# Forming the Strassen sums of w_out in the first phase and during the merges instead of in attention, and loading A11 of the out-projection during the last merge

## The chip, the cores and the metric

The kernel runs on one core of one Trainium2 chip. The metric is the device time of one execution in microseconds (us); several runs are taken and their median is given. The profile is of one execution, with a time of its own. Engines: PE (TensorE: matmuls; PEld its weight loads), DVE (VectorE), ACT (ScalarE), POOL (GpSimd), SP (SyncE, which issues all of this kernel's transfers, in one queue).

## The reference

One layer of a decoder trunk on 1024 tokens and 16 meta tokens, all in float32:

```python
h = rmsnorm(x, gain)
zin = h @ w_in.astype(h.dtype)                      # 2048 x 10240
q, k, v, g_attn, u, g_pool, m_attn, m_pool = jnp.split(zin, cuts, axis=-1)
o_attn = stick_breaking_attention(q, k, v).reshape(B, L, SB_WIDTH)
o_attn = (o_attn * jax.nn.silu(g_attn.astype(jnp.float32))).astype(x.dtype)
y_attn = o_attn @ w_attn_up.astype(x.dtype)         # 1024 x 2048
pooled = multiscale_pool(u.astype(jnp.float32))
mixed = jnp.einsum('blgc,gcd->blgd', pooled, pool_w.astype(jnp.float32)).reshape(B, L, POOL_WIDTH)
o_pool = (mixed * pool_scale.astype(jnp.float32) * jax.nn.silu(g_pool.astype(jnp.float32))).astype(x.dtype)
y_pool = o_pool @ w_pool_up.astype(x.dtype)         # 1024 x 2048
merged = jax.nn.sigmoid(m_attn) * y_attn + jax.nn.sigmoid(m_pool) * y_pool
return x + merged @ w_out.astype(x.dtype)           # 2048 x 2048
```

The layer's output goes through a last rmsnorm, and the meta tokens are dropped. The attention weights are `sigmoid(z) * product of (1 - sigmoid(z))` over the keys between, which the kernel forms by a running product (a scan) along the keys.

## The kernel before, in words

**Numbers.** Each float32 operand is split into a high and a low part (`split`, L115: ACT writes the high part at L116, DVE or POOL the rest at L117), and each product is three matmuls (`mm3`, L137, or L1007 to L1009): high x high, high x low, low x high. 512 columns are one matmul, so a block of 128 x 2048 by 2048 x 512 tokens is made of many of them.

**Products.** The two large projections, by w_in and by w_out, save multiplications in Strassen's manner: with each matrix cut in four, seven products of sums of quarters take the place of eight. So sums of quarters of the weights are needed (`make_sums`, L266, for w_in; `w_forms`, L183, for w_out), sums of quarters of the inputs, and sums of the results. Columns of w_in are worked on in pairs of 128, a `Duo` each; there are 40 of them.

**Stages**, by the profile's clock:

1. *First phase* (0 to about 985 us). The norm and the transposed input; six early duos; then the loop over `rest` (n = 0 to 33), in which each duo takes four of its seven products: by X0, X2, X1 and X3. For each duo the raw blocks of w_in are loaded (`load_raw`, L249, tiles raw0 with two buffers, raw1 and rawb with one each), POOL makes eight sums of them (L271), four of which go to DRAM (d_r, L280), and ACT and DVE split the others. Results go to DRAM as d_nu (L296, after X2), d_c or d_sa and d_sp (L314, after X1), d_up (L301, after X3). The pool p0 (small vectors of the norm and one tile `st` for early results) stays open for the whole phase; the pool wa (rawb, the sums, `st`, `tm`) lies beside it, over the memory of the pool px that is closed by then.
2. *Pooling* (to about 1170 us). The other three products of the pooling duos, the causal pooling and its group maps.
3. *Attention* (to about 1910 us). For each of eight heads the other three products of its two duos, and the attention itself as a generator that is advanced one step every few matmuls: scores, mask (L748 on POOL), scan (L753 on DVE), transpose (L769), values. Between them the remaining products of the 16 gate duos. `duo` and `silu_duo` call `between[0]` after each product; that advances `w_forms`.
4. *Merges* (to about 2275 us). 32 products of 128 output channels by the up-projections, in a written order of ("p", c) and ("a", c) pairs: the gate from DRAM is multiplied with the product (L965, L970), and the attention part added to the pool part on POOL (L971). When both halves of a channel pair are there, `sums` makes four sums (L949), and seven tiles go to DRAM (d_f, L957).
5. *Out-projection* (to the end). `prod` takes the seven products; A11 is loaded first, through the tile mr with two buffers (`fill_f`, L1013), the other operands (A12, R2, R3, and later R1, A22, R4) one block per step of the products before.

**w_forms before.** For each half p of w_out's columns, each of eight row blocks j and each half i of 512 columns it loads four blocks (tiles cw0 to cw3, 256 columns, 128 KB each), makes three of the four forms by subtractions on POOL (L194) and stores them (L195), loads two more blocks and makes the fourth: six loads, four subtractions, four stores, in three steps. 32 such units are spread over attention.

**Order of the work.** The framework orders the instructions of each engine by its own plan, not strictly by the source: what is ready may go ahead. `tc.keep_in_program_order` ties an instruction behind the one traced before it on its engine, so that it can't go ahead of that one; later ones can still go ahead of it. A new tile whose memory lay in a closed pool waits for the users of the tiles that were there (`reuse_waits="tile"`). A queue runs in the order that was planned, and an instruction that waits holds what is behind it.

Of the kernel before, what the change touches and what calls it, by code (L numbers as in the profile page):

```python
# [9 lines left out]
F32 = mybir.dt.float32  # L10
# [5 lines left out]
P = 128  # L16
D = 2048
KC = D // P
# [17 lines left out]
HALF = SEQ // 2  # L36
# [36 lines left out]
def trunk_kernel(  # L73
# [14 lines left out]
    nc = tc.nc  # L88
# [22 lines left out]
    def nm(s):  # L111
        uid[0] += 1
        return f"{s}_{uid[0]}"
# [66 lines left out]
    def w_form(n):  # L180
        return lambda p, j: d_wf[n][p][:, j * 512 : (j + 1) * 512]

    def w_forms(pool):  # L183

        for p, j, i in ((p, j, i) for p in range(2) for j in range(KH) for i in range(2)):
            c = slice(i * 256, (i + 1) * 256)

            def block_of(tag, kh, nh):
                t = pool.tile([P, 256], F32, tag=tag, name=nm("cw"), bufs=1)
                tc.keep_in_program_order(nc.sync.dma_start(t, w_block(p, j, kh, nh)[:, c]))  # L190
                return t

            def minus(n, a, b):
                tc.keep_in_program_order(nc.gpsimd.tensor_tensor(out=a, in0=a, in1=b, op=ALU.subtract))  # L194
                tc.keep_in_program_order(nc.sync.dma_start(w_form(n)(p, j)[:, c], a))  # L195
# [33 lines left out]
    with ExitStack() as actx:  # L229
# [15 lines left out]
        with ExitStack() as xctx:  # L245
# [68 lines left out]
                nc.sync.dma_start(dst, t)  # L314

            X0, X1 = xquads(0, XW), xquads(1, XW)
            p0 = xctx.enter_context(tc.tile_pool(name="p0", bufs=2, side="right", reuse_waits="tile"))
            gk = p0.tile([P, KC], F32, tag="gk", name="gk", bufs=1)
            early = ALL[:6]
            ops = {}  # L320
# [10 lines left out]
            with tc.tile_pool(name="px", bufs=1, side="right", reuse_waits="tile") as px:  # L331
# [94 lines left out]
                for d in early[1:]:  # L426
                    early_ops(d, 0)
                    a = acc_tile()
                    for kq in range(KQ):
                        block([a], WHOLE, X0, kq, ops[d.n, 0, kq], True)  # L430
                    s1 = wr_tile()
                    nc.scalar.activation(s1, a, AF.Copy)
                    nc.sync.dma_start(d_nu[d.n], s1)
                    early_ops(d, 1)
                    for kq in range(KQ):
                        block([a], WHOLE, X1, kq, ops[d.n, 1, kq], False)
                        if d.n < 5:
                            last_tokens(2 * (d.n - 1) + kq)
                    out_c(p0, 1, d, [a], WHOLE)
            nc.sync.dma_start(psc, pool_scale.rearrange("(c p) -> p c", p=P))  # L440

            wa = xctx.enter_context(tc.tile_pool(name="wa", bufs=1, side="right", reuse_waits="tile"))
# [58 lines left out]
            early_rest(early[0])  # L501
            raws = all_raws(rest[0])
            r2, r3 = make_sums(wa, rest[0], raws, SB)
            for n, d in enumerate(rest):
                pieces = WITHM if d.meta else WHOLE
                a, b = [acc_tile() for _ in pieces], acc_tile()
                for kq in range(KQ):
                    block(a, pieces, X0, kq, op_of(c0(raws[0][kq])), True)
                s1 = copy_p1(wa, STB, a, pieces)
                for kq in range(KQ):  # L510
                    block([b], WHOLE, X2, kq, op_of(r2[kq]), True)
                out_nu(wa, STB, d, s1, b)
                for kq in range(KQ):
                    block(a, pieces, X1, kq, op_of(c0(raws[1][kq])), False)
                out_c(wa, STB, d, a, pieces)
                m7 = [op_of(r3[kq]) for kq in range(KQ)]
                last = d is rest[-1]
                more = n + 1 < len(early)
                if not last and not more:
                    raws = all_raws(rest[n + 1])  # L520
                    r2, r3 = make_sums(wa, rest[n + 1], raws, SB)
                for kq in range(KQ):
                    block([b], WHOLE, X3, kq, m7[kq], False)
                out_up(wa, STB, d, s1, b)
                if more:
                    if n + 2 < len(early):
                        fetch_s1(early[n + 2])
                    early_rest(early[n + 1])
                    raws = all_raws(rest[n + 1])
                    r2, r3 = make_sums(wa, rest[n + 1], raws, SB)  # L530
                if 7 <= n < 7 + KC // 2:
                    second_operands(n - 7)
                if n == 7 + KC // 2:
                    second_meta()
                if 6 <= n < 6 + KC // 2:
                    fetch_x22(n - 6)

        def load_wr(src):
            raw = wp.tile([P, 512], F32, tag="wr", name=nm("wr"), bufs=4)
# [82 lines left out]

            return m5, n4, p3

        between = [lambda: None]

        def duo(*args):
            for call in duo_steps(*args):
                call()
                between[0]()  # L630

        def tok_tile(pool, tag, dt):

# [7 lines left out]
        with ExitStack() as a0ctx:  # L641
# [24 lines left out]
            def silu_duo(*args):  # L666
                for call in silu_steps(*args):
                    call()
                    between[0]()
# [51 lines left out]
        with tc.tile_pool(name="a1", bufs=1, side="right", reuse_waits="tile") as a1:  # L721
# [124 lines left out]
                duo(d, dst, post, None, step)  # L846

            gates = [d for d in ALL if d.kind in ("ma", "mp")]
            forms = w_forms(a1)
            between[0] = lambda: next(forms, None)  # L850
            for h in range(HEADS):
                d = named["kv", h]
                vT = tok_tile(a1, "vT", F32)
# [34 lines left out]
            for _ in att:  # L888
                pass
            gate_duo(gates.pop(0), None)  # L890
            for _ in forms:
                pass

    xo = ctx.enter_context(tc.tile_pool(name="xo", bufs=1, reuse_waits="tile"))
    xc = ctx.enter_context(tc.tile_pool(name="xc", bufs=1, side="right", reuse_waits="tile"))
# [10 lines left out]
    with tc.tile_pool(name="pm", bufs=2, side="right", reuse_waits="tile") as pm:  # L906
# [28 lines left out]
        for n, k in enumerate((("p", 0), ("p", KH), ("p", 1))):  # L935
            order.remove(k)
            order.insert(n, k)
        op, oa = [xquads(0, HALF, xo), xquads(1, HALF, xo)], [xquads(2, HALF), xquads(3, HALF, xc)]
        for t in range(2):
            fill_up(op[t], d_op, t)  # L940
# [2 lines left out]
        def sums(j):  # L943
# [9 lines left out]
            r3 = add(a11, a21)  # L953
            r2 = add(r1, a11)
            r4 = add(r2, a12)
            for n, t in enumerate((a11, a12, r2, r3, r1, a22, r4)):
                nc.sync.dma_start(d_f[n][j], t)  # L957

        for n, (kind, c) in enumerate(order):
            if n in (0, 1):  # L960
                fill_up(oa[n], d_oa, n)
            if kind == "p":
                gs = [gate("sp", 6, d_sp, c, t) for t in range(2)]
                for t, a in up_mm(w_pu, op, c):
                    nc.vector.tensor_tensor(out=gs[t], in0=a, in1=gs[t], op=ALU.mult)  # L965
                sps[c] = gs
            else:
                gs = [gate("sa", 6, d_sa, c, t) for t in range(2)]
                for t, a in up_mm(w_au, oa, c):
                    nc.vector.tensor_tensor(out=gs[t], in0=a, in1=gs[t], op=ALU.mult)  # L970
                    nc.gpsimd.tensor_tensor(out=gs[t], in0=gs[t], in1=sps[c][t], op=ALU.add)  # L971
                ms[c] = gs
                if c >= KH:
                    sums(c - KH)

    pr = ctx.enter_context(tc.tile_pool(name="pr", bufs=2, side="right", reuse_waits="tile"))
    rows = [[], []]
# [207 lines left out]
```

## Time and profile before

| | |
|---|---|
| time, median of three runs | 2611.47 us (2610.23 to 2613.19) |
| the profiled execution's own time | 2615.75 us |
| its span, from the first to the last instruction | 2614.0 us |
| mean granted clock of TensorE | 0.983 |
| busy: PE, DVE, ACT, POOL | 94%, 48%, 34%, 40% |
| DMA, mean over the span | 178 GB/s |

A busy share is the time in which the engine had an instruction in work, as a share of the span. The matmuls overlap, so that one is shown with about 0.39 us while the next starts 0.23 us later; what is lost on PE is seen in the stretches in which it has nothing in work. In the list of waits a row reads: who waited, for whom, total us, how many times, the longest. In a timeline: start, duration, engine, line, operation, output and inputs, count, and in brackets how long the engine had been idle and what ended that. SPq is the queue of transfers; its rows give the time of issuing, not of landing. In a chain of waits each row is a start, a length and what was on the path.

### The profile page before, as it was taken

How to read it: one execution, taken by the hardware profiler on the slowest of the kernel's cores; microseconds unless marked ns; L12 is line 12 of the kernel's file. 1: busy time of each engine (PE TensorE's matmuls, PEld its weight loads, DVE VectorE, ACT ScalarE, POOL GpSimd, SP SyncE). 2: the span in 40 equal slices, each digit the busy share in tenths (PEclk: the TensorE clock that was granted, in tenths of full speed). 3: DMA queues.
4: the chain of work that ended last, by engine and by line, in shares of the span. 5: the costliest groups of instructions: out<-in, count | busy, mean ns of one | idle time of the engine just before them, and what ended most of it. 6: DMA issues, size and time to landing. Idle time of an engine off the chain costs nothing. (4 is left out here: it accounts for less than half of the span.)

```text
span 2614.0 us, 36254 instructions
## 1 busy us (share of the span) xinstructions
PE 2468.5 (94%) x12680; PEld 2088.1 (80%) x12680; DVE 1253.8 (48%) x2089; ACT 896.0 (34%) x1845; POOL 1034.6 (40%) x962
## 2 busy tenths in 40 slices
PE   6898999999999999899999999999889999899998
PEld 5676778888888887887887888888768888677887
DVE  5432234543333344675575566557652222255456
ACT  6421122222222234224454454445441111044243
POOL 1665555554454534235445544554303222210212
PEclk8999999999999999999999999999989999999999
DMA  5566555665555557436556656554575444375544
GB/s 179 162 206 214 192 192 204 216 226 180 182 182 177 185 186 219 126 126 187 178 174 183 187 165 191 182 177 141 164 239 173 138 143 135 116 238 185 183 132 169
DMA packets 418168, 466.24 MB, mean 178 GB/s; under 512 B 35505, under 2 KB 278577, under 8 KB 416945
## 3 DMA queue, kind: packets, MB, share of 16 engines
q1 hardware_dynamic: 417984, 463.93, 55.8%
q8 instruction: 99, 1.62, 0.3%
q14 instruction: 85, 0.69, 0.1%
HBM read 321.50 MB, written 142.31 MB: 177 GB/s over the span
## 5 line engine op out<-in xcount | busy, mean ns | idle before, releaser
L138 PE MATMUL acc<-x,wh 128*128 128x512 f32 (+2 forms) x2736 | 980.2, 359 | 27.6 <-ACT wh L116 18.5
L140 PE MATMUL acc<-x,wl 128*128 128x512 f32 (+2 forms) x2736 | 971.1, 355 | 8.9 <-DVE wl L117 7.5
L139 PE MATMUL acc<-x,wh 128*128 128x512 f32 (+2 forms) x2736 | 968.8, 354 | 0.0
L138 PEld LDWEIGHTS acc<-x,wh 128*128 128x128 f32 x2736 | 520.1, 190 | 98.6 <-ACT wh L116 24.2
L140 PEld LDWEIGHTS acc<-x,wl 128*128 128x128 f32 x2736 | 518.6, 190 | 86.4 <-DVE wl L117 14.5
L139 PEld LDWEIGHTS acc<-x,wh 128*128 128x128 f32 x2736 | 519.3, 190 | 62.8
L116 ACT ACTIVATE wh<-wr 128x512 fp32r<-128x512 f32 x408 | 256.4, 630 | 580.6 <-PE accb L139 273.2
L117 DVE TENSOR_TENSOR wl<-wr,wh 128x512 fp32r<-128x512 f32 x288 | 217.2, 756 | 241.4 <-ACT wh L116 230.2
L117 DVE TENSOR_TENSOR wl<-r,wh 128x512 fp32r<-128x512 f32 x160 | 150.4, 944 | 339.3 <-ACT wh L116 315.2
L271 POOL TENSOR_TENSOR r<-raw,raw 128x512 f32<-128x512 f32 x80 | 111.7, 1396 | 378.8 <-DMA raw<-in_w_in_dram 357.0
L116 ACT ACTIVATE wh<-r 128x512 fp32r<-128x512 f32 x160 | 100.3, 632 | 469.7 <-POOL r L271 363.8
L117 POOL TENSOR_TENSOR wl<-wr,wh 128x512 fp32r<-128x512 f32 x120 | 171.8, 1431 | 224.0 <-ACT wh L116 170.6
L271 POOL TENSOR_TENSOR r<-r,raw 128x512 f32<-128x512 f32 x160 | 221.4, 1384 | 12.5 <-DMA raw<-in_w_in_dram 2.5
L138 PE MATMUL accb<-x,wh 128*128 128x512 f32 x512 | 200.5, 392 | 12.4 <-ACT x L116 12.4
L139 PE MATMUL accb<-x,wh 128*128 128x512 f32 x512 | 200.7, 392 | 0.0
L140 PE MATMUL accb<-x,wl 128*128 128x512 f32 x512 | 200.2, 391 | 0.0
L1007 PE MATMUL accb<-wh,x 128*128 128x512 f32 x416 | 163.8, 394 | 15.6 <-ACT x L116 13.3
L753 DVE TENSOR_TENSOR_SCAN wt<-wt 128x272 f32<-128x272 f32 (+5 forms) x128 | 109.8, 858 | 142.9 <-POOL wt L748 105.0
L194 POOL TENSOR_TENSOR cw<-cw,cw 128x256 f32<-128x256 f32 x128 | 106.1, 829 | 172.5 <-DMA cw<-in_w_out_dram 152.4
L1009 PE MATMUL accb<-wl,x 128*128 128x512 f32 x416 | 164.0, 394 | 2.5 <-DVE wl L117 2.3
L1008 PE MATMUL accb<-wh,x 128*128 128x512 f32 x416 | 163.3, 393 | 0.0
L971 POOL TENSOR_TENSOR sa<-sa,sp 128x512 f32<-128x512 f32 x32 | 47.2, 1475 | 275.4 <-DVE sa L970 265.9
(176 smaller groups left out, 3124.0 us busy)
## 6 DMA issues: line engine op xcount, KB each, us to landing
raw<-in_w_in_dram SPq DMA_DIRECT2D x96, 512.0 KB, 6.0
d_r<-r SPq DMA_DIRECT2D x160, 256.0 KB, 2.0
wr<-d_r SPq DMA_DIRECT2D x160, 256.0 KB, 3.3
raw<-in_w_in_dram SPq DMA_DIRECT2D x152, 256.0 KB, 5.3
cw<-in_w_out_dram SPq DMA_DIRECT2D x192, 128.0 KB, 3.2
wr<-in_w_in_dram SPq DMA_DIRECT2D x80, 256.0 KB, 3.0
d_wf<-cw SPq DMA_DIRECT2D x128, 128.0 KB, 2.0
wr<-d_wf SPq DMA_DIRECT2D x64, 256.0 KB, 2.8
```

Of the source, the lines that this page charges most:

```text
L116: nc.scalar.activation(hi, src, AF.Copy)
L117: (eng or nc.vector).tensor_tensor(out=lo, in0=src, in1=hi.bitcast(F32), op=ALU.subtract)
L138: nc.tensor.matmul(ps, wh, rh, start=first, stop=False, skip_group_check=skip)
L139: nc.tensor.matmul(ps, wh, rl, start=False, stop=False, skip_group_check=skip)
L140: nc.tensor.matmul(ps, wl, rh, start=False, stop=last, skip_group_check=skip)
L194: tc.keep_in_program_order(nc.gpsimd.tensor_tensor(out=a, in0=a, in1=b, op=ALU.subtract))
L271: nc.gpsimd.tensor_tensor(out=t, in0=a, in1=b, op=ALU.add)
L753: nc.vector.tensor_tensor_scan(out=rev, data0=rev, data1=rev, initial=wt[:, w : w + 1], op0=ALU.mult, op1=ALU.bypass)
L971: nc.gpsimd.tensor_tensor(out=gs[t], in0=gs[t], in1=sps[c][t], op=ALU.add)
L1007: nc.tensor.matmul(a, sh, wh, start=first and j == 0, stop=False, skip_group_check=not first)
L1008: nc.tensor.matmul(a, sl, wh, start=False, stop=False, skip_group_check=not first)
L1009: nc.tensor.matmul(a, sh, wl, start=False, stop=j == KH - 1, skip_group_check=not first)
```

## The change

`w_forms` takes the half p of the columns and the width n of a block as arguments. The half p = 0 is formed in the first phase, 256 columns at a time: a step after the product by X2 and a step after the product by X3 of each duo from n = 6 on. The half p = 1 is formed during the merges, 512 columns at a time, a step after each. Nothing of it is left in attention. The pool p0 is closed when the early duos are done, before wa is opened. In the merges the two gate tiles of the first merge are allocated and loaded ahead of the operands; the merged tiles that are operands themselves (forms 0, 1 and 5) are stored when they are ready and not with the sums; and after the last pool merge, ("p", 15), the operand A11 is allocated and loaded, through the tile ol of the merges with six buffers, while the last attention merge follows.

```diff
-    def w_forms(pool):
-
-        for p, j, i in ((p, j, i) for p in range(2) for j in range(KH) for i in range(2)):
-            c = slice(i * 256, (i + 1) * 256)
+    def w_forms(pool, p, n):
+        for j, i in ((j, i) for j in range(KH) for i in range(0, 512, n)):
+            c = slice(i, i + n)
...
-                t = pool.tile([P, 256], F32, tag=tag, name=nm("cw"), bufs=1)
+                t = pool.tile([P, n], F32, tag=tag, name=nm("cw"), bufs=1)
...
-            p0 = xctx.enter_context(tc.tile_pool(name="p0", bufs=2, side="right", reuse_waits="tile"))
+            p0ctx = ExitStack()
+            p0 = p0ctx.enter_context(tc.tile_pool(name="p0", bufs=2, side="right", reuse_waits="tile"))
...
                     out_c(p0, 1, d, [a], WHOLE)
+            p0ctx.close()
...
             r2, r3 = make_sums(wa, rest[0], raws, SB)
+            forms = w_forms(wa, 0, 256)
+
+            def between(n):
+                if n >= len(early):
+                    next(forms, None)
+
             for n, d in enumerate(rest):
...
                 out_nu(wa, STB, d, s1, b)
+                between(n)
...
                 out_up(wa, STB, d, s1, b)
+                between(n)
...
+            for _ in forms:
+                pass
...
-        between = [lambda: None]
-
         def duo(*args):
             for call in duo_steps(*args):
                 call()
-                between[0]()
...
-            forms = w_forms(a1)
-            between[0] = lambda: next(forms, None)
...
-            for _ in forms:
-                pass
...
+        first = [gate("sp", 6, d_sp, 0, t) for t in range(2)]
         op, oa = [xquads(0, HALF, xo), xquads(1, HALF, xo)], [xquads(2, HALF), xquads(3, HALF, xc)]
...
-            for n, t in enumerate((a11, a12, r2, r3, r1, a22, r4)):
+            for n, t in ((2, r2), (3, r3), (4, r1), (6, r4)):
                 nc.sync.dma_start(d_f[n][j], t)
 
+        forms = w_forms(pm, 1, 512)
         for n, (kind, c) in enumerate(order):
...
-                gs = [gate("sp", 6, d_sp, c, t) for t in range(2)]
+                gs = [gate("sp", 6, d_sp, c, t) for t in range(2)] if n else first
...
                 ms[c] = gs
+                nc.sync.dma_start(d_f[c // KH][c % KH], gs[0])
                 if c >= KH:
+                    nc.sync.dma_start(d_f[5][c - KH], gs[1])
                     sums(c - KH)
+            next(forms, None)
+            if (kind, c) == ("p", KC - 1):
+                for _ in forms:
+                    pass
+                A11 = xquads(0, HALF, xo)
+                for j in range(KH):
+                    fill(A11, j, d_f[0][j])
...
-    A11, A12 = xquads(0, HALF, xo), xquads(1, HALF, xo)
-    for call in fills((A11, 0)):
-        call()
+    A12 = xquads(1, HALF, xo)
```

More of the change, by code (lines that the diff above doesn't have):

```diff
@@ L181, in w_form, with minus @@
         return lambda p, j: d_wf[n][p][:, j * 512 : (j + 1) * 512]
-    def w_forms(pool):
-        for p, j, i in ((p, j, i) for p in range(2) for j in range(KH) for i in range(2)):
-            c = slice(i * 256, (i + 1) * 256)
+    def w_forms(pool, p, n):
+        for j, i in ((j, i) for j in range(KH) for i in range(0, 512, n)):
+            c = slice(i, i + n)
             def block_of(tag, kh, nh):
-                t = pool.tile([P, 256], F32, tag=tag, name=nm("cw"), bufs=1)
+                t = pool.tile([P, n], F32, tag=tag, name=nm("cw"), bufs=1)
                 tc.keep_in_program_order(nc.sync.dma_start(t, w_block(p, j, kh, nh)[:, c]))
                 return t
-            def minus(n, a, b):
+            def minus(f, a, b):
                 tc.keep_in_program_order(nc.gpsimd.tensor_tensor(out=a, in0=a, in1=b, op=ALU.subtract))
-                tc.keep_in_program_order(nc.sync.dma_start(w_form(n)(p, j)[:, c], a))
+                tc.keep_in_program_order(nc.sync.dma_start(w_form(f)(p, j)[:, c], a))
                 return a
@@ L668, in silu_duo @@
                     call()
-                    between[0]()
             def sil_tiles():
```

## The prediction

> **What bounds the kernel now.** I read the busy times by stage first, then the list of waits in the stage that idles, then the chain of waits at its two ends, and last the queue of transfers in the first phase.
>
> Busy time of each engine by stretch (columns: stretch, length, PE, PEld, DVE, ACT, POOL, granted clock, DMA share, GB/s):
>
> ```profile
> 335.00:985.00 650.00, 649.89 (x3397) 561.91 (x3396) 264.39 (x345) 179.09 (x342) 325.31 (x234) 1.00 0.59 192
> 664.80:675.70 10.90, 10.90 (x72) 10.03 (x71) 2.56 (x4) 1.96 (x5) 10.66 (x8) 1.00 0.27 101
> 675.70:686.70 11.00, 11.00 (x72) 10.13 (x71) 4.43 (x7) 3.39 (x8) 0.02 (x2) 1.00 0.89 261
> 1170.00:1909.90 739.90, 703.34 (x4124) 610.46 (x4122) 450.91 (x911) 354.59 (x838) 345.36 (x460) 1.00 0.57 175
> 1909.90:1922.50 12.60, 0.20 (x2) 0.01 (x1) 1.32 (x3) 1.94 (x4) 0.93 (x2) 0.72 0.58 186
> 1922.50:1929.00 6.50, 6.50 (x15) 4.82 (x16) 4.87 (x8) 4.35 (x7) 0.00 (x0) 0.50 0.84 277
> 1929.00:2274.30 345.30, 345.30 (x1523) 285.20 (x1521) 100.06 (x151) 53.83 (x87) 81.05 (x59) 1.00 0.48 152
> 2274.30:2287.80 13.50, 0.24 (x2) 0.04 (x1) 1.34 (x3) 1.33 (x3) 6.60 (x5) 0.61 0.59 198
> 2287.80:2294.30 6.50, 6.50 (x15) 4.86 (x16) 3.11 (x5) 2.46 (x4) 0.00 (x0) 0.50 0.83 277
> ```
>
> TensorE is never idle in the steady first phase (335 to 985) and in the merges (1929 to 2274). It loses 739.9 - 703.3 = 36.6 us in attention (1170 to 1910), and stands still twice: 12.4 us between attention and merges, 13.3 us between merges and out-projection. After each standstill the granted clock is 0.50 for 6.5 us, 3.25 us more. The change reaches for these three losses, and pays in the two stages that lose nothing.
>
> **Attention: removed work.** The sums leave attention whole. What they do there, from the waits in that window (who waits, for whom, us, times, longest) and the queues at one head:
>
> ```profile
> POOL cw L194 <- DMA cw<-in_w_out_dram: 145.3, 52, 8.0
> ```
> ```profile
> DVE wt L753 <- POOL wt L748: 105.0, 58, 7.8
> ```
> ```profile
> DVE wt L753 <- ACT wt L743: 37.6, 45, 1.8
> ```
> ```profile
> PE tr L769 <- DVE bt L754: 15.1, 8, 3.4
> PE tr L769 <- DVE wt L751: 11.2, 9, 2.1
> PE tr L769 <- DVE aT L117: 6.6, 12, 0.8
> ```
> ```profile
> 1303.75 0.72 POOL L194 TENSOR_TENSOR cw<-cw,cw 128x256 f32<-128x256 f32 x1 [3.70 <-issue]
> 1304.43 0.29 POOL L748 TENSOR_SCALAR_AFFINE_SELECT wt<-wt 128x128 f32<-128x128 f32 x1
> ```
>
> POOL stands in its queue before a subtraction whose block has not landed, the mask (L748) stands behind it, the scan (L753) waits for the mask, the transpose (L769) for the scan. The transposes wait 15.1 + 11.2 + 6.6 = 32.9 us. Of the scan's own waits 105.0 of 142.6 us (74%) are for POOL, the rest for ACT, which this change leaves alone. 0.74 x 32.9 = 24 us come back. Ends: 32.9 (all of it) and 0 (the scan's latency alone keeps the transposes waiting).
>
> **First standstill.** SP's queue between attention and merges; the chain of waits runs through these rows and POOL's last subtraction:
>
> ```profile
> 1912.41 1.16 SPq L190 DMA_DIRECT2D cw<-in_w_out_dram  x2
> 1917.88 0.33 SPq L195 DMA_DIRECT2D d_wf<-cw  x1
> 1918.31 13.81 SPq L910 DMA_DIRECT2D ol<-d_op  x16
> ```
>
> The first operand load (ol) stood in SP's queue behind the last form's store, which waited for POOL, which waited for a load. Without it the load can issue at 1912.4, 5.9 us earlier; that is the lower end. The change also allocates the gate tiles ahead of the ol tiles, so that ol no longer falls on the memory of the tiles that the last gate writes; if the loads then start under the last product, all 12.4 + 3.25 = 15.7 us go. I take 10, between the two: some wait stays, since the gate loads, now ahead in the source, lie over the last product's inputs.
>
> **Second standstill.** SP's queue, and the end of the chain of waits:
>
> ```profile
> 2278.37 4.10 SPq L957 DMA_DIRECT2D d_f<-r  x4
> 2282.57 0.40 SPq L124 DMA_DIRECT2D wr<-in_w_out_dram  x1
> 2283.06 0.88 SPq L1015 DMA_DIRECT2D mr<-d_f  x2
> ```
> ```profile
> 2283.06 4.00 DMA mr<-d_f
> 2287.06 0.02 issue
> 2287.09 0.64 ACT x L116
> ```
>
> The load of A11 stands in SP's queue behind the stores of the last four sums. After the change it follows the last pool merge, one attention merge earlier: 48 matmuls x 0.2265 us (345.3 us / 1523) = 10.9 us of cover. One fill is 4.00 + 0.64 + about 0.7 = 5.3 us; eight fills trail by DVE's 0.7 each, and the product needs one each 2.7 us. So the standstill shrinks to some 1.5 us: 13.3 + 3.25 - 1.5 = 15 us. Ends: 8 (fills late) and 16.5. The later fills (A12, R2, R3) keep their pace.
>
> The clock after a standstill has a rule in the Trainium skill, TensorE: Matmul & The Clock Gate, Part 1, What's actually happening: half rate after an idle window of about 3.4 us, full rate after a busy one. The rows above agree in kind (0.50 after 12 us of idleness) but show 6.5 us of it, near two such windows. By that rule a rest of 4 us at the first standstill could keep 3.25 of the 10 us.
>
> **First phase: added work.** Half of the sums (16 units of six loads, four subtractions and four stores) go between the products of the duos from n = 6 on, two thirds of a unit in each of 24 duos. Prices from the tile cw (min/median/max ns):
>
> ```profile
> L190 SPq DMA_DIRECT2D cw<-in_w_out_dram x192: 327/422/1733, 1174.7 to 1913.2; - x192
> L194 POOL TENSOR_TENSOR cw<-cw,cw x128: 723/742/1271, 1179.3 to 1917.1; 128x256 f32<-128x256 f32 x128
> ```
>
> Per duo: 6.7 issues x 0.42 = 2.8 us of SP, 2.7 subtractions x 0.74 = 2.0 us of POOL, 6.7 x 131 KB = 0.87 MB of traffic. What it meets, POOL's and SP's queues over one duo:
>
> ```profile
> 686.69 1.30 POOL L271 TENSOR_TENSOR r<-raw,raw 128x512 f32<-128x512 f32 x1 [10.98 <-DMA raw<-in_w_in_dram]
> ```
> ```profile
> 672.17 0.38 SPq L296 DMA_DIRECT2D d_nu<-st  x1
> 675.73 0.32 SPq L280 DMA_DIRECT2D d_r<-r  x1
> 676.15 0.99 SPq L257 DMA_DIRECT2D raw<-in_w_in_dram  x2
> 677.56 0.34 SPq L314 DMA_DIRECT2D d_c<-st  x1
> 678.01 1.10 SPq L257 DMA_DIRECT2D raw<-in_w_in_dram  x2
> 679.20 0.57 SPq L301 DMA_DIRECT2D d_up<-st  x1
> 679.86 3.31 SPq L257 DMA_DIRECT2D raw<-in_w_in_dram  x4
> ```
>
> POOL sums for 10.9 us (664.8 to 675.7), then waits 11 us for the next raw blocks, whose loads are issued only after the store of its last sum (676.15 after 675.73) and fill the DMA to 0.89. That ring takes 21.9 us, and TensorE's 96 matmuls take 96 x 0.2265 = 21.7: the ring is hidden with nothing to spare, and I count no slack. POOL's 2.0 us fit in its 11 us of waiting. The traffic is what counts: in the stretch of sums the DMA is at 0.27 and it is free; in the stretch of raw loads it lengthens the ring, at 261 GB/s by 0.87 / 0.261 = 3.3 us. Upper end: 24 x 3.3 = 79 us; lower end 0. A form's transfers are pinned behind the store before them in the source: behind d_nu (672.17, in the stretch of sums: free) or behind d_up (679.20, among the raw loads). Of the second half only what gets ahead of the third raw block delays POOL's first sum; I take half. So a quarter counts: 0.83 us x 24 = 20 us lost.
>
> The Trainium skill has a rule that speaks against this move: DMA: Bandwidth & Descriptors, Issuing engines are not separate DMA queues, says that all transfers run on the same 16 engines and interleave. The row with share 0.89 agrees. By that page's 341 GB/s for 1 MB an estimate of the upper end would be 0.87 / 0.341 x 24 = 61 us.
>
> **The early close of p0.** The tiles of wa then lie over p0, whose tile st holds the last early result:
>
> ```profile
> 120.95 2.64 POOL L271 TENSOR_TENSOR r<-raw 128x512 f32<-128x512 f32 x2 [1.79 <-PE xtr L374]
> ```
> ```profile
> 121.74 3.96 SPq L257 DMA_DIRECT2D raw<-in_w_in_dram  x2
> ```
> ```profile
> 138.63 0.52 SPq L314 DMA_DIRECT2D d_sp<-st  x1
> ```
>
> The first row shows such a wait today (a sum in wa waits for the transposes that read the old tile). The raw block at 121.74 would wait for the store at 138.63, 17 us later, once. Other products can go first; I take 6 us lost, ends 0 and 17.
>
> **Merges: added work.** Eight units of 512 columns: 48 loads, 32 stores, 32 subtractions of about 1.3 us (a form's 0.74 us at 256 columns, under twice that at 512). POOL is busy 81 of 345 us there, the DMA at 0.48; 42 us of POOL fit. The stores of merged tiles move up one by one. If a late subtraction holds POOL for its longest wait (8.0 us) a merge is late, but eight PSUM banks of 5.4 us stand between. I take 1 us, ends 0 and 8.
>
> **Sum.** 24 + 10 + 15 - 20 - 6 - 1 = 22 us off the span of 2614.0: 2592. The profiled run took 2615.75, 1.75 more than its span and 4.3 more than the median of the runs (2611.47), so 2592 + 1.75 - 4.3 = 2589.5, told as 2589.
>
> **Rivals.**
> 1. The ring becomes TensorE's bound in the first phase. Gains of 49 less 7 leave 42, so it decides from 42 / 24 = 1.75 us per duo on, a little over half of the traffic ahead of the sums. For it: no spare time in the ring. Against: POOL and DMA idle for half of each duo. With three quarters, 2.5 us x 24 = 60 lost, 18 more than the gain: slower, 2629; with all of it, 79: 2648.
> 2. The first phase hides everything: 2589 - 20 = 2569. For it: DMA at 0.27 in every stretch of sums.
> 3. The masks come early and the transposes wait all the same, for scan, product and split: attention gives some 6 of 24, 2607. For it: 37.6 us of scan waits on ACT. Against: at 1303.75 POOL had been waiting 3.70 us.
>
> **How the numbers follow.** Forecast 0.45 (its own range 2576 to 2603), rival 1 0.18, rival 2 0.25, rival 3 0.12. The range runs from 2560 (rival 2 with the upper ends at both standstills, 15.7 and 16.5, and a little of the p0 cost saved) to 2629 (rival 1). A measurement of this kernel can tell about 0.2%, 5 us. Forecast and rival 2 are faster, rival 3 half faster and half the same, rival 1 slower up to a small part: faster 0.74, same 0.08, slower 0.18.
>
> **What would show it.** Right: no cw row in attention, the scan's wait for POOL far below 105 us, TensorE's idle time in attention near 13 us; a standstill under 2 us before L1007 and no half clock behind it, about 3 before the merges; the first phase some 20 us longer, with TensorE waiting on wh or wl from r. Wrong: TensorE idle over 40 us between 400 and 985, with the raw loads landing later after POOL's last sum; transposes waiting as long as now; or a stall of over 10 us near 140.

## The result, and the profile after

The changed kernel takes 2628.2 us (median of 4 runs, 2625.7 to 2631.0); the kernel before took 2610.9 us beside it (4 runs, 2608.5 to 2613.2). The ratio is 1.0067, 95% interval 1.0049 to 1.0084: slower by 0.7%, where 0.8% faster was forecast. The profiled execution spans 2629.3 us against 2614.0.

Both kernels issue the same 12,680 matmuls in the same order, so the stages can be cut at the same matmul. The table gives the time between the starts of the matmuls that bound each stage.

| stage | before | after | change | predicted |
|---|---|---|---|---|
| start to the 1510th matmul (early close of p0) | 397.5 | 400.5 | +3.0 | +6 |
| first phase, to the 4634th | 587.9 | 647.2 | +59.3 | +20 |
| pooling, to the 5586th | 184.9 | 183.7 | -1.2 | 0 |
| attention, to its last matmul | 739.3 | 709.6 | -29.7 | -24 |
| first standstill | 12.8 | 10.0 | -2.8 | -10 with its half clock |
| merges | 351.6 | 350.8 | -0.8 | +1 |
| second standstill | 13.7 | 0.2 | -13.5 | -15 with its half clock |
| out-projection to the end | 326.3 | 327.3 | +1.0 | 0 |

The changes add up to +15.3, the difference of the spans. One row decides: the first phase. Busy times by stretch of the kernel after (columns as in the prediction):

```profile
400.50:1047.70 647.20, 613.79 (x3126) 517.54 (x3125) 238.27 (x316) 160.01 (x314) 332.53 (x271) 0.98 0.65 206
1231.40:1940.90 709.50, 698.91 (x4120) 611.54 (x4119) 453.15 (x911) 354.26 (x838) 232.64 (x333) 1.00 0.41 124
1940.90:1951.00 10.10, 0.51 (x4) 0.08 (x2) 1.35 (x3) 1.95 (x4) 0.00 (x0) 0.73 0.73 236
1951.00:1957.50 6.50, 6.50 (x18) 4.88 (x19) 5.31 (x8) 4.64 (x8) 0.00 (x0) 0.63 0.85 270
1957.50:2301.80 344.30, 344.30 (x1520) 284.64 (x1519) 109.14 (x158) 58.63 (x95) 124.94 (x91) 1.00 0.68 217
2328.90:2334.60 5.70, 0.42 (x2) 0.00 (x0) 1.60 (x2) 3.35 (x6) 4.31 (x4) 1.00 0.89 316
```

TensorE, never idle in the first phase before, now is idle for 33.4 us of it (647.2 - 613.8), and the granted clock falls to 0.98. Note the DMA share: 0.65, hardly above the 0.59 of before. On the average of the stage the transfers do not fill the DMA engines. The list of waits of SP's queue between 400 and 985 us has a line that the kernel before has not:

```profile
SPq L191 <- DMA d_wf<-cw: 30.1, 8, 4.8
```

A load of a block (L191, which was L190) waited for a form's store to land, 8 times, 3.8 us each, in every third duo. SP's queue in one of these duos, after POOL's last sum:

```profile
787.05 0.33 SPq L281 DMA_DIRECT2D d_r<-r  x1
787.47 1.57 SPq L258 DMA_DIRECT2D raw<-in_w_in_dram  x2
...
790.16 1.19 SPq L258 DMA_DIRECT2D raw<-in_w_in_dram  x2
791.43 0.46 SPq L302 DMA_DIRECT2D d_up<-st  x1
791.98 0.38 SPq L196 DMA_DIRECT2D d_wf<-cw  x1
792.42 6.62 SPq L191 DMA_DIRECT2D cw<-in_w_out_dram  x4
799.13 2.03 SPq L258 DMA_DIRECT2D raw<-in_w_in_dram  x4
```
```profile
803.62 1.29 POOL L272 TENSOR_TENSOR r<-raw,raw 128x512 f32<-128x512 f32 x1 [0.95 <-DMA raw<-in_w_in_dram]
```

The last difference of a unit is stored from the tile cw1 (791.98). The next unit starts with four loads, the second of them into cw1, which has one buffer. It must wait until that store has landed, and the store runs among the raw loads. Four issues, 1.7 us at 0.42 each, take 6.62, and the last four raw loads stand behind them: they are issued 12.1 us after the d_r store, where before the change it was about 4 (675.73 and 679.86 in the prediction). POOL's first sum starts at 803.6, 27.4 us after the one of the duo before; the next two duos take 21.8 and 24.2. The sum at 803.62 waited 0.95 us for its raw block when POOL's subtractions ahead of it were done, so here the load came last and not POOL.

### The profile page after: what moved, and what is told of

Its sections match the earlier page's. It is cut to its first block, busy times and chain, and to the rows that moved or that the text cites. A ratio compares the mean times of both kernels' runs of the same rounds, so it can differ in the third digit from the quotient of the medians.

```text
span 2629.3 us, 36031 instructions
## 1 busy us (share of the span) xinstructions
PE 2488.4 (95%) x12680; PEld 2094.0 (80%) x12680; DVE 1254.9 (48%) x2089; ACT 895.0 (34%) x1845; POOL 1006.8 (38%) x930
## 4 chain that ended last, share of the span: by engine, by line
PE 54%; DMA 12%; POOL 12%; DVE 7%; issue 5%; ACT 2%; SPq 2%; POOLq 0%; DVEq 0%; ACTq 0%
POOL r L272 11%; PE acc L140 9%; PE acc L139 9%; PE acc L138 9%; DMA raw<-in_w_in_dram 7%; PE accb L138 4%; PE accb L139 4%; PE accb L140 4%; PE accb L1026 3%; PE accb L1024 3%; PE accb L1025 3%; DVE wl L117 2%; DMA mr<-d_f 2%; DMA d_wf<-cw 1%; ACT wh L116 1%
## 5 line engine op out<-in xcount | busy, mean ns | idle before, releaser
L195 POOL TENSOR_TENSOR cw<-cw,cw 128x256 f32<-128x256 f32 (+1 forms) x96 | 96.1, 1001 | 281.4 <-DMA cw<-in_w_out_dram 278.1
L763 DVE TENSOR_TENSOR_SCAN wt<-wt 128x272 f32<-128x272 f32 (+5 forms) x128 | 107.6, 841 | 110.2 <-POOL wt L758 65.1
L116 ACT ACTIVATE wh<-raw 128x512 fp32r<-128x512 f32 x160 | 97.1, 624 | 135.9 <-PE acc L139 84.2
```

Source lines behind the costliest of these rows:

```text
L116: nc.scalar.activation(hi, src, AF.Copy)
L763: nc.vector.tensor_tensor_scan(out=rev, data0=rev, data1=rev, initial=wt[:, w : w + 1], op0=ALU.mult, op1=ALU.bypass)
```

## The experiments

Stages are named as in the table; "first phase" is the time from the 1510th to the 4634th matmul, 587.9 us before and 647.2 after. Three explanations stood at the start: A, the order of SP's one queue (waits and issues ahead of the raw loads); B, the bytes of the forms on the DMA engines; C, the subtractions ahead of the sums in POOL's queue.

**1. two_buffers.** Against after:

```diff
-                t = pool.tile([P, n], F32, tag=tag, name=nm("cw"), bufs=1)
+                t = pool.tile([P, n], F32, tag=tag, name=nm("cw"), bufs=2 if (tag, n) == ("cw1", 256) else 1)
```

> One change against the kernel after: in the first phase the tile cw1, from which the last difference of a unit is stored and into which the next unit's second block is loaded, has two buffers instead of one. Bytes, subtractions and places stay. Theory A (the order of SP's queue): in the trace of the kernel after, SP's loads of cw wait 30.1 us in 8 waits for a store of cw to land, with the raw loads behind them; without these waits about 27 of the some 59 us that the first phase lost come back: 2601 us, and the ring of 26.7 us in every third duo falls to 24 or less. Theory B (the bytes themselves fill the 16 DMA engines): nothing changes, 2628. Theory C (the subtractions stand in POOL's queue before the sums): nothing changes, 2628.

Measured: 2590.6 us, ratio to before 0.9915 (0.9898 to 0.9932). First phase 610.7: 36.5 of the 59.3 us are gone with the same bytes and subtractions. SP's queue in the same kind of duo:

```profile
763.75 0.38 SPq L196 DMA_DIRECT2D d_wf<-cw  x1
764.18 2.29 SPq L191 DMA_DIRECT2D cw<-in_w_out_dram  x4
766.83 2.37 SPq L258 DMA_DIRECT2D raw<-in_w_in_dram  x4
```

The four issues take 2.29 us. The 36.5 us are more than the 30.1 of the waits themselves, because the one buffer also moved loads. Where a unit's four loads follow d_nu, the queue of the kernel after has only the first of them ahead of the last d_r store:

```profile
834.07 0.45 SPq L191 DMA_DIRECT2D cw<-in_w_out_dram  x1
836.73 0.32 SPq L281 DMA_DIRECT2D d_r<-r  x1
837.15 0.39 SPq L258 DMA_DIRECT2D raw<-in_w_in_dram  x1
837.63 1.48 SPq L191 DMA_DIRECT2D cw<-in_w_out_dram  x3
```

The other three run among the raw loads, in seven duos, 21 loads in all; in two_buffers all four stand ahead of the d_r store. So of the forms' 160 transfers in SP's queue 101 stand between a duo's last d_r store and its last raw load in the kernel after, and 80 in two_buffers. At 0.30 us for a load there (experiment 4) the 21 are some 6 us, an estimate; with the 30.1 that makes 36. Both parts go with the one buffer, so A, the order of SP's queue, is shown for the 36.5 us; some 6 of them are bytes that the order had moved. 22.8 us stay.

**2. two_buf_nosubs**, for what stays: two_buffers without the `gpsimd.tensor_tensor` of the first phase.

> two_buffers without the subtractions of the first phase: the loads and the stores stay, and the blocks are stored as they were loaded (the sums of that half are left out). It splits the 22.7 us that the first phase of two_buffers still loses (610.7 against 588.0). Theory C (POOL: subtractions that wait for a late block and then stand before the sums; in two_buffers every third duo has three of them right before the sums, and takes 23.4 us instead of 22): most of it comes back, first phase under 598. Theory A and B (issues and bytes among the raw loads): it stays above 604.

Measured: 2596.8 us (one run), first phase 613.6, no shorter than 610.7. C is out for what stays: in two_buffers the subtractions cost nothing.

**3. placed, spread, mixed, mixed_up.** All keep the fourth difference in a fifth tile, so that a unit has eight transfers, and differ in where its steps stand:

```python
# spread: two loads | two loads | four subtractions and their stores; one step at each
#         of the two places, behind d_nu and behind d_up; 16 units
# placed: behind d_nu all loads and stores, behind d_up the subtractions; 16 units
# mixed:  as spread, but only behind d_nu; 8 units; 12 blocks of 512 columns in the merges
# mixed_up: mixed, with its steps behind d_up in place of d_nu
```

> The first phase keeps its half of the sums, but in another order: a fifth tile takes the fourth difference, so that nothing is loaded twice (8 transfers of 128 KB a unit, not 10); all loads and stores of a unit go behind the store of d_nu, in the stretch of sums, and the four subtractions behind the store of d_up, after POOL's last sum. Theory A (SP's queue between the last d_r store and the raw loads): no transfer of the forms is left among the raw loads, the ring goes back to about 22 us, the first phase loses under 8 us: 2575 us. Theory B (bytes): 16.8 instead of 21 MB, so about 0.8 of the 59 us stays: 2616. Theory C (POOL): the four subtractions, 3 us, still stand before the next sums: 2620 or more.

Measured: 2605.4 us, ratio 0.9966 (0.9955 to 0.9977), first phase 626.1. A miss. The loads are behind d_nu in the source, but three of the four go into tiles, of one buffer each, whose stores stand right before them, and only the stores went ahead of the last d_r store. The loads stand in front of all raw loads, or of all but one:

```profile
734.17 1.93 SPq L524 DMA_DIRECT2D d_wf<-cw  x4
737.29 0.32 SPq L281 DMA_DIRECT2D d_r<-r  x1
737.71 0.38 SPq L258 DMA_DIRECT2D raw<-in_w_in_dram  x1
738.19 1.94 SPq L512 DMA_DIRECT2D cw<-in_w_out_dram  x4
...
741.13 1.86 SPq L258 DMA_DIRECT2D raw<-in_w_in_dram  x3
```

The stage loses 38.2 us, more than the 32 that the 8.4 MB of the 64 loads take at 261 GB/s. What of it is theirs, and what the four subtractions', which stand right before the sums here, no run shows.

> In the first phase a fifth tile takes the fourth difference, so that no block is loaded twice (8 transfers a unit instead of 10), and a unit is spread over three steps: two loads, two loads, four subtractions with their stores; no tile is loaded within half a duo of its last store. Against two_buffers (first phase 610.7 us, 22.7 lost): Theory A and B both expect a fifth less of what is left, 606 us, 2586; theory C (POOL): four subtractions in a row, 3 us, stand before the sums in every third half duo, no gain or a loss: 2591 or more.

Measured: 2587.4 us, ratio 0.9889 (0.9871 to 0.9908), first phase 605.9, as expected of A and B.

> Five tiles in both places: four of the sixteen column blocks in the first phase (8 units of 256 columns, three steps each, one step a duo, always behind d_nu), twelve in the merges (two steps each, one behind each product, 24 steps as in the kernel after). First phase: half of the work of spread, which lost 18 us, and no step behind d_up among the raw loads: 594 us. Merges: 24 steps cost nothing in the kernel after, 352 us. 2575 us by theory A and B; by theory C (POOL's four subtractions in a row before the sums in every third duo) first phase 600, 2581.

Measured: 2571.9 us, ratio 0.9836 (0.9814 to 0.9857), first phase 589.2, merges 352.5. Half of spread's units lose 1.3 us where spread lost 18.

> As mixed, with one difference: the step of each duo in the first phase stands behind the store of d_up, among the raw loads, instead of behind the store of d_nu. Same units, same bytes, same subtractions. If the place decides: mixed lost 1.3 us in the first phase, and here nearly all of the loss per step that two_buffers and spread showed comes back, 18 us x 8/16 units or more: first phase 598 to 604 us, 2583. If the amount decides (spread has twice the units): 589 to 591, 2572.

Measured: 2590.0 us, ratio 0.9896 (0.9869 to 0.9924), first phase 605.1. The same units, half a duo later, lose 17.2 us. Busy times over the first phase of mixed, then of mixed_up:

```profile
400.50:989.70 589.20, 588.30 (x3125) 510.83 (x3124) 257.74 (x316) 163.29 (x315) 328.01 (x242) 1.00 0.64 205
```
```profile
399.50:1004.60 605.10, 596.43 (x3126) 510.38 (x3125) 244.90 (x316) 159.53 (x314) 318.89 (x242) 1.00 0.62 200
```

The DMA moves as much and more per us in the kernel that loses nothing. The place decides, not the amount: behind d_nu the step is free, behind d_up it pays.

**4. extra_full, extra_small.** What does a transfer among the raw loads cost by, issue or bytes? Both add to merges_five (below; no sums in its first phase) two loads, w = 256 or 16:

```diff
                 out_up(wa, STB, d, s1, b)
+                if n >= len(early):
+                    for m in range(2):
+                        t = wa.tile([P, w], F32, tag=f"ex{m}", name=nm("ex"), bufs=1)
+                        tc.keep_in_program_order(nc.sync.dma_start(t, w_block(0, n % KH, m, 0)[:, :w]))
```

> merges_five, whose first phase has no sums, with two loads of 128 x 256 (131 KB each) added behind d_up in each of the duos from n = 6 on, into tiles that nobody reads. No store, no subtraction and no wait of one for the other: only transfers among the raw loads. By their bytes: 0.26 MB / 261 GB/s = 1.0 us a duo; by their issue: 2 x 0.42 = 0.84 us a duo. Either way the first phase gets some 15 to 24 us longer, 604 to 613 us, as far as the ring has no slack; 2590 us.

> As extra_full, with loads of 128 x 16 (8 KB each) in the same places: the issues stay, the bytes are a sixteenth. If the issue in SP's queue is what a transfer among the raw loads costs: as long as extra_full, within 4 us. If the bytes are: first phase 589 to 593 us, 2576.

Measured: extra_full 2592.0 us, ratio 0.9914 (0.9891 to 0.9937), first phase 604.0; extra_small 2567.9, ratio 0.9823 (0.9800 to 0.9846), first phase 589.5. The loads in the list of transfers from 400 to 985 us (count, KB each, median us to landing), of extra_full and of extra_small:

```profile
ex<-in_w_out_dram SPq DMA_DIRECT2D x52, 128.0 KB, 5.0
```
```profile
ex<-in_w_out_dram SPq DMA_DIRECT2D x52, 8.0 KB, 4.9
```

The same issues, 54 in the first phase (52 of them in the window of the list), cost some 16 us with 131 KB each and under 2 us with 8 KB. So it is the bytes that cost: 7.1 MB at 261 GB/s are 27 us, of which 0.6 counted, or 0.30 us a load. At that price the 80 transfers that two_buffers has behind d_up come to 24 us, and it lost 22.8; the 64 of spread and of mixed_up come to 19, and they lost 18.0 and 17.2. What two_buffers left is B: bytes among the raw loads. The Trainium skill, DMA: Bandwidth & Descriptors, Issuing engines are not separate DMA queues, says that all transfers share the same 16 engines and that another issuer saves issue time only. These two runs agree in that the bytes cost and the issues hardly do (16 and under 2 us); they have no other issuer.

**5. pool_stores.** Against two_buffers, `nc.sync.dma_start` of the forms' stores becomes `nc.gpsimd.dma_start`.

> As two_buffers, with the stores of all forms issued from POOL's queue instead of SP's. In two_buffers the first phase still loses 22.7 us (610.7 against 588.0). Theory A (what is left is SP's order too): 2.7 issues of 0.45 us and their waits for POOL leave SP's queue per duo, some 1.2 us of 24 duos come back in part: first phase 600 us, 2581 us. Theory B (bytes) and C (the subtractions before the sums): unchanged, 2591; if a store's issue takes POOL over 1 us, it is later than 2591.

Measured: 2607.6 us, ratio 0.9969 (0.9954 to 0.9985), first phase 625.3, 14.6 longer than two_buffers. POOL's queue where three subtractions stand before the sums:

```profile
708.32 0.85 POOL L195 TENSOR_TENSOR cw<-cw,cw 128x256 f32<-128x256 f32 x1 [8.48 <-DMA cw<-in_w_out_dram]
709.47 0.56 POOL L196 DMA_DIRECT2D d_wf<-cw  x1 [0.30 <-POOL cw L195]
...
713.30 1.31 POOL L272 TENSOR_TENSOR r<-raw,raw 128x512 f32<-128x512 f32 x1
```

A subtraction with its store takes POOL 1.7 us instead of 0.8 (0.30 of rest and 0.56 of issue more); three of them fill 5.0 us in front of the sums, and the sum at 713.30 starts without a wait for its raw block. There C becomes true; whether that is all of the 14.6 us no run shows.

**6. p0_att.** The first phase's half goes back to attention, as in the kernel before; the rest as after.

> The first phase's half of the sums goes back to attention, between the products as in the kernel before; the other half stays in the merges, the first operand of the out-projection is still loaded during the last merge, and the early tiles are still freed early. All theories: the first phase goes back to its time before (59 us less, the 3 us near 140 us stay), attention gives back about half of its gain of 30 us: 2628 - 59 + 15 = 2584 us. It prices the first-phase part by itself; a first phase still longer than 655 us between 335 and 985 would mean that something else than the sums lengthens it.

Measured: 2588.1 us, ratio 0.9902 (0.9887 to 0.9917). First phase 588.0: nothing but the sums lengthens it. Attention 730.3: one half of the sums costs 20.7 us there (730.3 - 709.6), the second half only 9.0 more.

**7. Where else: all_merges, merges_pool, merges_five, p0_pooling.**

```python
# all_merges:  forms of p = 0 and 1 in the merges, two steps behind each product
# merges_pool: all_merges, stores issued by POOL, cw1 with two buffers
# merges_five: five tiles; four loads | four subtractions and stores; one step behind each product
# p0_pooling:  p = 0 between the products of the pooling stage, two steps behind each
```

> Both halves of the sums go in the merges (two steps of the list behind each merge), none in the first phase or in attention; the rest as in the kernel after. Theory A (what costs is transfers in the one queue where a loop waits for its loads, and the merges have no such loop): 2628 - 59 = 2569 us, merges within 5 us of 351. Theory B (bytes): the merges' DMA share, 0.48 without and 0.68 with one half, would come to some 0.88, as high as in the first phase's raw loads, and the merges lose 20 us or more: 2590. POOL: 81 us of its own and 32 x 4 / 2 subtractions of about 1.4 us, 90 us, fit in 350 in any case.

Measured: 2618.9 us, ratio 1.0029 (1.0012 to 1.0047), merges 401.7. TensorE and SP's queue in the merges (waits), and the busy times, with a granted clock of 0.94:

```profile
PE accb L138 <- ACT wh L116: 31.7, 8, 12.2
```
```profile
SPq L196 <- POOL cw L195: 143.8, 62, 5.5
```
```profile
1886.70:2288.40 401.70, 369.28 (x1536) 297.48 (x1537) 121.57 (x166) 63.23 (x102) 164.56 (x123) 0.94 0.74 243
```

> All sums in the merges as in all_merges, with two edits: the stores of the forms are issued from POOL's queue, right behind the subtraction that makes them, and cw1 has two buffers. In the trace of all_merges SP waits 143.8 us in 62 waits for POOL before a form's store and 13.3 us for a store to land, with the weight loads behind, TensorE waits 31.7 us for weights, and the merges last 402 us instead of 351. Theory A (the order of SP's queue): the merges go back to 351 to 357 us, 2570 us. Theory B (bytes: DMA share 0.74 over 402 us would be 0.85 over 351): the merges stay above 385 us, 2605 or more. A new wait would be POOL's own: the issue of a store on POOL has no row yet.

Measured: 2624.5 us, ratio 1.0035 (1.0019 to 1.0050), merges 401.7 again. POOL's wait left SP's queue, and another took its place:

```profile
SPq L191 <- DMA d_wf<-cw: 72.1, 21, 6.9
```

> All sums in the merges, with the five tiles of spread: 8 transfers a unit, nothing loaded twice, two steps a unit (four loads; four subtractions and their stores), and one step behind each merge product instead of two. Against all_merges (merges 402 us) 33.5 MB instead of 41.9, and each product meets at most four transfers. Theory A (what counts is how long SP's queue stands before a store or a load between two products' weights): merges 352 to 362 us, 2574 us. Theory B (bytes: share about 0.78 over 351 us against 0.69 of the kernel after, which loses nothing): also near 355. It would be wrong if the four loads, which wait for the stores of the step before, hold the weight loads up: 380 us or more, 2600.

Measured: 2574.8 us, ratio 0.9845 (0.9829 to 0.9862), merges 352.3 with all the sums in them. The waits for POOL before a store, and the busy times of the merges:

```profile
SPq L965 <- POOL cw L964: 43.1, 38, 2.7
```
```profile
1900.70:2253.20 352.50, 351.48 (x1536) 289.21 (x1537) 124.86 (x166) 62.67 (x102) 168.56 (x123) 0.99 0.77 250
```

At a share of 0.77 and 250 GB/s nothing is lost, at 0.74 in all_merges 50 us were. That B doesn't bind at the higher share is shown; that A does in all_merges rests on the waits, since merges_five also moves a fifth less.

> The first phase's half of the sums goes into the pooling stage between the first phase and attention (two steps behind each product), the rest as in the kernel after. The stage lasts 181.5 us without sums (all_merges), with TensorE idle for some 17 us of it and the DMA at 0.51. All theories: first phase as in the kernel before (59 us less). Theory A: the stage has weight loads in SP's queue that the forms' stores hold up, as in the merges at two steps a product: it loses 10 to 25 us, 2585. Theory B (bytes: 21 MB more over 182 us are 115 GB/s on top of 157): 272 GB/s is as high as the first phase's loads reach, it loses about as much. If neither binds, 2567.

Measured: 2621.0 us, ratio 1.0021 (1.0008 to 1.0033); the stage takes 229.0 us, 45 more than after, and attention 717.4, 8 more, well beyond the loss expected (5.3 of the 8 are one wait of TensorE for DVE that the kernel after has not). The wait that leads SP's list in the stage is the one of all_merges:

```profile
SPq L196 <- POOL cw L195: 82.0, 56, 5.2
```

**8. five_p0open**, merges_five with p0 open to the end of the first phase.

> merges_five with the pool p0 of the early products open until the first phase ends, as in the kernel before: the tiles of wa lie beside its tiles and not over them. If the early close costs what the prediction put at 6 us (0 to 17): the point at which the 1510th product starts, 398 us before and 396 to 409 in the kernels with the close, comes 3 to 9 us earlier, 2569 us. If it costs nothing: 2575, and the spread of that point has another cause.

Measured: 2567.4 us, ratio 0.9815 (0.9794 to 0.9836), by its median the fastest kernel here (extra_small and mixed lie within the intervals), 1.9% below before and, by the two ratios, 2.5% below after. Its 1510th matmul starts at 395.6, that of merges_five at 407.0. But with the early close that point lay anywhere from 396 to 409 in the profiles of the 15 kernels that have it (mean 400), and the intervals of the two ratios overlap. A cost of a few us is likely; its size stays open.

## Why the prediction was wrong, step by step

**First phase (20 predicted, 59.3 measured): a step was missing.** The working sorted the forms' transfers into those behind d_nu, free, and those behind d_up, of which half counts. Both prices hold where the queue keeps that order: mixed lost 1.3 us behind d_nu; mixed_up lost 17.2 behind d_up, about half of the 32 us that its 8.4 MB take at 261 GB/s; and two_buffers, with half of its transfers in each place, lost 22.8 us, 0.95 a duo, where 0.83 was forecast. The "quarter" was right, 22.8 of 80 us at 261 GB/s. What the working lacked was a wait: it costed each load at its issue of 0.42 us and never asked what a load waits for. A load into a tile with one buffer waits for that tile's store to land, and what stands behind it in SP's queue was listed there: the raw loads, in a ring without slack. The same buffer undid "behind d_nu: free" for 21 loads, which the queue had among the raw loads. Waits (30.1 us) and moved loads (some 6, the estimate above) were together worth the 36.5 us. Rival 1 came about in its kind: the ring became the bound. But its reason, three quarters of the traffic ahead of the sums, was not the main cause: 101 of 160 transfers ran among the raw loads, where 80 were expected, and the waits cost some five times what those 21 did. That its 2629 meets the 2628.2 is luck.

**Attention (24 predicted, 29.7 measured): right, a little low.** The waits of TensorE and of the scan in that window of the kernel after:

```profile
PE tr L779 <- DVE wt L761: 7.0, 9, 1.6
PE tr L779 <- DVE aT L117: 1.0, 2, 0.6
```
```profile
DVE wt L763 <- POOL wt L758: 65.1, 64, 2.7
```

The transposes wait 8.0 instead of 32.9 us. The scan's wait for POOL fell only from 105.0 to 65.1 us, so the 0.74 by which the gain was scaled was no measure; its longest wait fell from 7.8 to 2.7, which may be what mattered; no run separates it. Rival 3 is out.

**First standstill (10 predicted, 5.9 to 15.7; 2.8 of rest and 0.8 in the merges measured): outside its bounds.** The end of the chain of waits there, after the change:

```profile
1942.01 0.70 DVE wl L117
1942.72 0.37 SPq L124
1943.18 0.46 SPq L854
1943.69 0.42 SPq L937
1944.16 0.47 SPq L937
1944.68 5.58 DMA ol<-d_op
```

The step "Without it the load can issue at 1912.4, 5.9 us earlier" took the form's store for the last thing in front of the load. Next in the queue stood a weight load that waits for its buffer (until 1942.7), the last gate's store and the two gate loads that the change itself moved ahead. The load was issued 3.7 us after the last product's last matmul started (1940.98), against 8.6 before: 4.9 us gained; and 6.3 us passed from there to the first merge matmul against 4.2, with gates and weights on the same DMA (0.73): 2.1 given back.

**Second standstill (15 predicted, 12.5 measured: 13.5 us of rest less 1.0 us in the out-projection).** It vanished as forecast, 13.7 to 0.2, and with it the 3.25 us of half clock behind it, but 27 us later there is a new wait, first as TensorE has it, then in SP's queue:

```profile
2334.66 0.79 PE L1024 MATMUL accb<-wh,x 128*128 128x512 f32 x1 [5.34 <-ACT wh L116]
```
```profile
2328.51 0.33 SPq L1032 DMA_DIRECT2D mr<-d_f  x1
...
2329.36 0.43 SPq L124 DMA_DIRECT2D wr<-in_w_out_dram  x1
```

A weight block of the second product (2329.36) stood in the queue behind the fills of A12 (mr), each of which waits for one of two buffers. "The later fills (A12, R2, R3) keep their pace" was the step that failed: at their pace, as the rows read, they now hold up the weights, because TensorE starts 13.5 us sooner.

**Early close and merges (6 and 1 predicted).** The early close measured 3.0, within its ends of 0 and 17, but is not settled, as said. The merges' added work cost nothing: they took 0.8 us less, which is what the clock gave at their start (0.63 in place of 0.50 over 6.5 us).

With what the one buffer cost added, 36.5 us, the forecast of 2589 would have been 2625. Without it the change is faster: two_buffers is the same change, at 2590.6. That this lies so near to 2589 is in part luck: attention's term was 5.7 us too small, the first standstill's 6.4 too large.

## What to carry to other kernels

Where a queue that feeds a loop without slack gets new transfers, write down for each load which earlier store or reader frees its tile, and what stands behind it: a tile with one buffer that is stored and then loaded turns an issue of 0.4 us into a wait for a landing, for everything behind, and the planned order may put the loads that follow it elsewhere than the source does. Put such transfers where the loop's own loads are not in flight (here behind d_nu), read in the trace whether the queue has them there, and keep a store that waits for another engine to few and short stops. A wait that is removed shows the next one in the same queue: look what stands there before the gain is counted.

## What was not expected of the hardware

TensorE ran at half pace after short rests. The kernel after, in the duo whose sums stand at 654:

```profile
662.14 0.40 PE L140 MATMUL acc<-x,wl 128*128 128x512 f32 x1
664.36 0.50 PE L138 MATMUL acc<-x,wh 128*128 128x512 f32 x1 [1.82 <-ACT wh L116]
664.69 0.40 PE L139 MATMUL acc<-x,wh 128*128 128x512 f32 x1
665.60 0.79 PE L140 MATMUL acc<-x,wl 128*128 128x512 f32 x1 [0.51 <-DVE wl L117]
666.19 0.63 PE L138 MATMUL acc<-x,wh 128*128 128x512 f32 x1
```

After rests of 1.82 and 0.51 us the matmuls follow each other at 0.43 us for some 3 us (until 668.75), where 0.23 is usual; the granted clock from 665.60 to 668.80 was 0.50. In two_buffers, at 502.5 us, rests of 1.76 and 0.51 us were followed by no such stretch; there TensorE had worked without a rest from 495.8 on, while the kernel after had two more rests, of 0.84 and 0.38 us, in the 7 us before 664.36. The Trainium skill, TensorE: Matmul & The Clock Gate, Part 1, What's actually happening, puts half rate after an idle window of about 3.4 us; here the two rests and the work between them took 3.1 us (662.5 to 665.6), the rests alone 2.3, and the longest single rest 1.82, so that half rate came without one idle stretch of that length. Worked out from the starts of the matmuls, the first phase of after loses 38.8 us in 34 rests of over 0.5 us and some 11 us in 56 matmuls that follow at about twice the usual distance. As the ring was the bound, this half pace may have filled time in which TensorE would have rested; no run separates the two. And a load of 8 KB among the raw loads took as long to land as one of 131 KB, 4.9 and 5.0 us.
